# Keeping the split input-projection weights of a decoder layer in DRAM after the first token tile

## The chip, the cores and the metric

The kernel runs on one core of a Trainium2 chip. The metric is the device time of one execution in microseconds (us). A core has five engines, each with an instruction stream of its own that runs in order: TensorE (PE in the profile, its weight loads PEld), VectorE (DVE), ScalarE (ACT), GpSimd (POOL) and SyncE (SP), which here issues nearly all DMAs between DRAM and the on-chip memories. Streams meet at semaphores. An instruction that waits holds up everything behind it in its own stream, and for SP that means every later DMA.

## The reference, cut to what matters

The reference is one decoder layer on 2048 tokens of width 1024, in float32. What the change touches is the input projection; what follows it is shown so that the stages can be named.

```python
mod = c_act @ w_ada[l] + b_ada[l]
shift_a, scale_a, gate_a, shift_f, scale_f, gate_f = jnp.split(mod[:, None, :], N_MOD, axis=-1)
h = x * (1.0 + scale_a) + shift_a
proj = h @ w_in                       # (2048, 1024) @ (1024, 3088)
sb_q, sb_k, sb_v, g_q, g_k, g_v, g_lr, g_r = jnp.split(proj, split_at, axis=-1)
# group A: stick-breaking attention, 8 heads x 64
w = jnp.where(causal, jnp.exp(log_beta + tail), 0.0)
# group B: gated linear attention, 4 heads, chunks of 64
o = jnp.concatenate([o_sb, o_gla], axis=-1) @ w_out
x = layer_norm(DEEPNORM_ALPHA * x + (1.0 + gate_a) * o, ln1_g, ln1_b)
h = x * (1.0 + scale_f) + shift_f
x = layer_norm(DEEPNORM_ALPHA * x + (1.0 + gate_f) * conv_glu_ffn(h), ln2_g, ln2_b)
```

## The kernel before

**Products in two parts.** Every float32 operand of a large product is split into a high part, rounded to the matmul's format, and a low part, which is the rest. A product is then three matmuls into one PSUM bank: high by high, high by low, low by high (`col_tile`, L267 to L269, with the weights stationary, and `row_tile`, L276 to L278, with the tokens stationary).

**How a weight is split.** `weights` (L162) loads up to 1024 elements a partition of a weight (four blocks of 128 rows by 256 columns, 512 KB) into a tile `w_raw`, of which there are three. `split` (L156) has ACT copy it to `w_hi` with a cast (L158) and POOL subtract to make `w_lo` (L159, engine `pool`). ACT, DVE and POOL instructions that go through the helper `Urgent` carry line L101 in the profile. `ring_pair` (L147) hands out the pairs `w_hi`, `w_lo`: four pairs that are used in turn, so a pair is written again when the matmuls that read it are done. A 256-column group of `w_in` takes two pairs.

**Tiles and stages.** The 2048 tokens go in four tiles of 512. For each tile the whole of `w_in` is loaded and split: 11 groups of 256 columns in two parts each and one group of 272 columns in three (`C_GV + 256` to `C_LR + 16`), 25 parts a tile and 100 in all. Tile 0's projections (`projections(0)`, L806) stand at the start, beside the sums that make shift and scale from `w_ada`. Then `attend(t)` (L471), the stick-breaking attention of tile t, is interleaved with `between(t)`: the linear attention of tile t (`gla`, L543, with its own four groups of `w_in`), the gate (`gla_gate`, L677) and the projections of tile t+1 (`proj_sb`, L435). `spread` (L789) decides by costs such as `WP` how far the one goes for each step of the other. Beside them run the rest of the `w_ada` sums (`ada_rest`, L280, on DVE) and `scale_w_out` (L307), which makes both parts of `w_out` and stores them in DRAM; `load_w_out` (L319) later loads them straight into ring pairs. The last attention runs beside the output projection (`mixer_out`, L721). The feed-forward part starts near 1,600 us and its order stands apart from `w_in`.

**The attention step** works on 128 queries by 512 keys: two matmuls (L494, L495), two sigmoids on ACT (L496, L497), a scan on DVE (L508), a product on DVE or POOL (L510), four transposes on PE (L518), a cast on ACT (L522), a subtraction on DVE (L523) and two matmuls (L524, L526).

**What sets the order.** The program is written stage by stage, and a scheduler then places every instruction in its engine's stream by a timeline that it estimates. A change in the durations or the number of instructions moves rows on all engines as far as the stages allow.

Of the kernel before, what the change touches and what calls it, by code (L numbers as in the profile page):

```python
# [19 lines left out]
F32 = mybir.dt.float32  # L20
# [8 lines left out]
P = 128  # L29
TQ = 512  # L30
NB = TQ // P
D = 1024
KT = D // P
# [49 lines left out]
C_SBQ, C_SBK, C_SBV, C_GQ, C_GK, C_GV, C_LR, C_GR = 0, 512, 1024, 1536, 1792, 2048, 2560, 2576  # L83


def layer(tc, x, c, w_ada, b_ada, w_in, gla_w_gate, gla_b_gate, sb_norm_g, gla_norm_g, w_out,
          ln1_g, ln1_b, w_ff_gate, w_ff_up, conv_w, conv_b, w_down, ln2_g, ln2_b, out):
    nc = tc.nc
# [15 lines left out]
    act, dve, pool = Urgent(nc.scalar), Urgent(nc.vector), Urgent(nc.gpsimd)  # L104
# [3 lines left out]
    w_ada, w_in, w_out = w_ada[0], w_in[0], w_out[0]  # L108
# [6 lines left out]
    dram = ctx.enter_context(tc.tile_pool(name="dram", bufs=1, space=DRAM))  # L115
# [31 lines left out]
    def ring_pair():  # L147

        pool, size = ext.get("pool"), ext.get("size", 0)
        i = ext.get("i", 0)  # L150
        ext["i"] = (i + 1) % (4 + size)
        if i < 4:
            return [wring.tile([P, 1024], F32R, name=f"w_{n}", bufs=4) for n in ("hi", "lo")]
        return [pool.tile([P, 1024], F32R, name=f"w_{n}x", bufs=size) for n in ("hi", "lo")]

    def split(raw, n, nw, lo_eng):  # L156
        hi, lo = (w[:, 0:1024 // nw * nw].rearrange("p (k c) -> p k c", c=nw) for w in ring_pair())
        act.copy(hi[:, 0:n], raw[:, 0:n])  # L158
        lo_eng.tensor_sub(lo[:, 0:n], raw[:, 0:n], hi[:, 0:n])  # L159
        return hi, lo  # L160

    def weights(src, lo_eng, nk=KT, scale=None):  # L162

        nw = src.shape[-1]
        per = 1024 // nw
        parts = []
        for k0 in range(0, nk, per):
            n = min(per, nk - k0)
            raw = wring.tile([P, 1024], F32, name="w_raw", bufs=3)
            raw = raw[:, 0:per * nw].rearrange("p (k c) -> p k c", c=nw)  # L170
            nc.sync.dma_start(raw[:, 0:n], src[k0 * P:(k0 + n) * P, :].rearrange("(k p) c -> p k c", p=P))
            if scale is not None:
                pool.tensor_mul(raw[:, 0:n], raw[:, 0:n], scale.unsqueeze(1).to_broadcast([P, n, nw]))
            parts.append(split(raw, n, nw, lo_eng))
        return parts

    def load_x(t):
        xt = []
        for tb in range(NB):
            xx = pj.tile([P, D], F32, name="t4k", bufs=4)  # L180
            nc.sync.dma_start(xx, x[t * TQ + tb * P:t * TQ + (tb + 1) * P, :])
            xt.append(xx)
        return xt

    with tc.tile_pool(name="ada", bufs=1, reuse_waits="tile") as ada:
# [34 lines left out]
        w_first = [[], []]  # L220
        done = 0
        for n in FIRST:
            ada_cols(KT + done, n, wa_first if done == 0 else None)
            ada_cols(done, n)
            cs = slice(done * P, (done + n) * P)
            for tb in range(NB):
                nc.sync.dma_start(x_first[tb][:, cs], x[tb * P:(tb + 1) * P, cs])
            if done % 4 == 0 and (done == 0 or not WLATE):
                for w, c0 in zip(w_first, (C_SBQ, C_SBK)):
                    w += weights(w_in[done * P:(done + 4) * P, c0:c0 + 256], pool, 4)  # L230
            done += n
        if WLATE:
            for w, c0 in zip(w_first, (C_SBQ, C_SBK)):
                w += weights(w_in[512:D, c0:c0 + 256], pool, 4)
        gmask_f = ada.tile([P, P], F32, name="gmask_f")
        nc.vector.memset(gmask_f, 1.0)
        nc.gpsimd.affine_select(gmask_f, gmask_f, pattern=[[1, P]], compare_op=ALU.is_ge, fill=0.0,
# [197 lines left out]
    def proj_sb(t, h):  # L435
        hh, hl = h
        for g in range(2):
            for kind, c0, dst in (("q", C_SBQ, dq), ("k", C_SBK, dk)):
                first = t + g == 0
                w = w_first[c0 // 512] if first else weights(w_in[:, c0 + 256 * g:c0 + 256 * (g + 1)], pool)  # L440
                for half in range(2):
                    if first:
                        ps = ps_first.pop(0)
                    else:
                        ps = psm.tile([P, TQ], F32, name="acc", bufs=3)
                        col_tile(ps, w, half, hh, hl)
                    hi = pj.tile([P, TQ], F32R, name="ev_hi", bufs=2)
                    lo = pj.tile([P, TQ], F32R, name="ev_lo", bufs=2)
                    if kind == "q":
                        act.mul(hi, ps, 0.125)  # L450
                        dve.scalar_tensor_tensor(lo, ps, 0.125, hi, ALU.mult, ALU.subtract)
                    else:
                        act.copy(hi, ps)
                        dve.tensor_sub(lo, ps, hi)
                    p = 2 * g + half
                    nc.sync.dma_start(dst[p][t][0], hi.bitcast(F32))
                    nc.sync.dma_start(dst[p][t][1], lo.bitcast(F32))
                    yield WP
            w = weights(w_in[:, C_SBV + 256 * g:C_SBV + 256 * (g + 1)], pool)
            for tb in range(NB):  # L460
                ps = psm.tile([P, TQ], F32, name="acc", bufs=3)
                row_tile(ps[:, 0:256], w, tb, hh, hl)
                v2 = pj.tile([P, 4, P], F32R, name="ev_v", bufs=2)
                pv = ps[:, 0:256].rearrange("p (h d) -> p h d", d=64)
                act.copy(v2[:, :, 0:64], pv)
                dve.tensor_sub(v2[:, :, 64:P], pv, v2[:, :, 0:64])
                nc.sync.dma_start(dv[g][t][:, tb], v2.bitcast(F32))
                if tb % 2:
                    yield WP
# [73 lines left out]
    def gla(t, h):  # L543
        hh, hl = h
        vn = pj.tile([P, NB, 512], F32, name="vn")
        w = weights(w_in[:, C_GV + 256:C_LR + 16], pool)
        for tb in range(NB):
            ps = psm.tile([P, TQ], F32, name="acc", bufs=3)
            row_tile(ps[:, 0:272], w, tb, hh, hl)
# [4 lines left out]
        with tc.high_priority(offset=400):  # L554
# [12 lines left out]
            m = pj.tile([P, 2, TQ], F32, name="t4k", bufs=4)  # L567
# [7 lines left out]
            act.activation(m, u, AF.Exp, scale=1.0 / 16)  # L575
            act.activation(u, u, AF.Exp, scale=-1.0 / 16)
        eb, enb = m, u
        w = weights(w_in[:, C_GV:C_GV + 256], pool)
        for tb in range(NB):
            ps = psm.tile([P, TQ], F32, name="acc", bufs=3)  # L580
            row_tile(ps[:, 0:256], w, tb, hh, hl)
            act.copy(vn[:, tb, 0:256], ps[:, 0:256])
            if tb % 2:
                yield WP
        wq = weights(w_in[:, C_GQ:C_GQ + 256], pool)
        wk = weights(w_in[:, C_GK:C_GK + 256], pool)
        cores = []
        for g in range(2):
            ps = psm.tile([P, TQ], F32, name="acc", bufs=3)
# [87 lines left out]
    def gla_gate(t, h, heads):  # L677
        hh, hl = h
        for hd in heads:
            if hd % 2 == 0:  # L680
                w = weights(w_in[:, C_GR + P * hd:C_GR + P * hd + 256], pool)
            ps = psm.tile([P, TQ], F32, name="acc", bufs=3)
            col_tile(ps, w, hd % 2, hh, hl)
            sg = pj.tile([P, TQ], F32, name="t2k", bufs=2)
            act.activation(sg, ps, AF.Sigmoid)
            dve.scalar_tensor_tensor(sg, ps, cols[:, R_GLG + hd:R_GLG + hd + 1], sg, ALU.mult, ALU.mult)
            nc.sync.dma_start(dsr[hd][t], sg)
            yield WP
# [416 lines left out]
    first = len(units) - NFF  # L1105
# [105 lines left out]
```

## Time and profile before

| | us |
|---|---|
| median of 3 runs (lowest, highest) | 3020.49 (3019.66, 3026.47) |
| the profiled execution's own time | 3018.13 |
| its span, first to last instruction | 3016.4 |
| its mean granted TensorE clock | 0.955 |

The page of the profile gives busy time by engine, the span in 40 slices of 75.4 us, DMA queues, the chain of waits that ended last, groups of instructions and DMA issues. A group's row reads: line, engine, operation, what it writes and reads, partitions by elements, count, busy us and mean ns of one, and after a second bar, where there is one, how long the engine stood idle just before these instructions and who ended that. A row of a windows table reads: from and to in us, length, busy us of each engine with its count of instructions, granted clock, mean busy share of the 16 DMA engines, GB/s. Times of a stretch are counted from the span's start.

### The profile page before, as it was taken

How to read it: one execution, taken by the hardware profiler on the slowest of the kernel's cores; microseconds unless marked ns; L12 is line 12 of the kernel's file. 1: busy time of each engine (PE TensorE's matmuls, PEld its weight loads, DVE VectorE, ACT ScalarE, POOL GpSimd, SP SyncE). 2: the span in 40 equal slices, each digit the busy share in tenths (PEclk: the TensorE clock that was granted, in tenths of full speed). 3: DMA queues.
4: the chain of work that ended last, by engine and by line, in shares of the span. 5: the costliest groups of instructions: out<-in, count | busy, mean ns of one | idle time of the engine just before them, and what ended most of it. 6: DMA issues, size and time to landing. Idle time of an engine off the chain costs nothing.

```text
span 3016.4 us, 37763 instructions
## 1 busy us (share of the span) xinstructions
PE 2789.2 (92%) x13387; PEld 2246.3 (74%) x13387; DVE 2060.3 (68%) x2829; ACT 1168.0 (39%) x1910; POOL 1219.6 (40%) x1202
## 2 busy tenths in 40 slices
PE   7998999989898998989886999988999997999998
PEld 6877877777787775667655788876888886888887
DVE  6466568688888779798547776767666665335665
ACT  2544354475566656544212333333222333112111
POOL 3554345477585545465425434453343430000000
PEclk9998999999999998988988999999999998999999
DMA  7755555546464335557763244344222336444553
GB/s 248 229 174 178 160 156 153 187 147 180 133 216 123 91 121 174 182 185 232 249 227 96 80 129 130 91 133 126 81 81 84 84 98 227 131 131 157 168 169 128
DMA packets 364710, 457.48 MB, mean 152 GB/s; under 512 B 21518, under 2 KB 257256, under 8 KB 364520
## 3 DMA queue, kind: packets, MB, share of 16 engines
q1 hardware_dynamic: 362216, 446.66, 47.7%
q0 software_dynamic: 2304, 8.39, 0.7%
q8 instruction: 106, 1.74, 0.2%
q14 instruction: 84, 0.69, 0.1%
HBM read 356.39 MB, written 98.57 MB: 151 GB/s over the span
## 4 chain that ended last, share of the span: by engine, by line
PE 66%; DVE 18%; DMA 5%; issue 4%; ACT 3%; POOL 2%; SPq 1%; POOLq 0%; DVEq 0%; ACTq 0%
PE acc L396 6%; PE acc L394 6%; PE acc L395 6%; DVE pp L508 5%; PE acc L974 4%; PE acc L972 4%; PE acc L973 4%; PE acc L101 3%; PE acc L268 3%; PE acc L267 3%; PE acc L269 2%; PE wt L518 2%; PE wt L972 2%; PE wt L973 2%; PE wt L974 2%
## 5 line engine op out<-in xcount | busy, mean ns | idle before, releaser
L508 DVE TENSOR_TENSOR_SCAN pp<-pp,beta 128x512 f32<-128x512 f32 (+2 forms) x320 | 408.8, 1291 | 55.7 <-ACT beta L497 27.5
L101 POOL TENSOR_TENSOR w_lo<-w_raw,w_hi 128x1024 fp32r<-128x1024 f32 (+2 forms) x108 | 265.1, 2460 | 256.1 <-ACT w_hi L101 230.6
L101 ACT CAST w_hi<-w_raw 128x512 fp32r<-128x512 f32 (+3 forms) x248 | 201.4, 830 | 353.3 <-PE acc L973 87.3
L510 POOL TENSOR_TENSOR beta<-beta,pp 128x512 f32<-128x512 f32 (+2 forms) x160 | 200.2, 1252 | 244.2 <-DVE pp L508 205.6
L101 POOL TENSOR_TENSOR w_lo<-wsum,w_hi 128x1024 fp32r<-128x1024 f32 x80 | 207.0, 2587 | 220.3 <-ACT w_hi L101 192.5
L972 PE MATMUL acc<-t,w_hi 128*128 128x512 f32 x640 | 251.2, 394 | 22.9 <-ACT t L101 21.3
L974 PE MATMUL acc<-t,w_lo 128*128 128x512 f32 x640 | 247.3, 393 | 8.0 <-DVE w_lo L101 8.0
L973 PE MATMUL acc<-t,w_hi 128*128 128x512 f32 x640 | 251.5, 393 | 1.6 <-DVE t L101 1.4
L394 PE MATMUL acc<-t,ah 128*128 128x512 f32 x576 | 225.2, 391 | 16.3 <-ACT ah L101 16.3
L523 DVE TENSOR_TENSOR wl<-wt,wh 128x512 fp32r<-128x512 f32 (+1 forms) x320 | 185.4, 597 | 65.0 <-ACT wh L522 63.3
L101 ACT CAST ah<-al 128x1408 fp32r<-128x1408 f32 x64 | 88.1, 1377 | 363.5 <-PE acc L395 359.6
L396 PE MATMUL acc<-t,al 128*128 128x512 f32 x576 | 225.2, 391 | 0.4 <-DVE al L101 0.4
L395 PE MATMUL acc<-t,ah 128*128 128x512 f32 x576 | 225.0, 391 | 0.0
L522 ACT CAST wh<-wt 128x512 fp32r<-128x512 f32 (+1 forms) x320 | 162.1, 530 | 158.7 <-PE wt L518 146.7
L496 ACT ACTIVATE pp<-z 128x512 f32<-128x512 f32 (+2 forms) x320 | 173.8, 544 | 124.7 <-PE z L495 58.6
L518 PE MATMUL wt<-ident,beta 128*128 128x128 f32 x1088 | 189.1, 294 | 13.2 <-DVE beta L510 8.5
L267 PE MATMUL acc<-hh,w_hi 128*128 128x512 f32 x480 | 194.7, 406 | 4.8 <-DVE ev_lo L101 2.5
L268 PE MATMUL acc<-hl,w_hi 128*128 128x512 f32 x480 | 191.5, 399 | 3.4 <-DVE hl L101 3.4
L269 PE MATMUL acc<-hh,w_lo 128*128 128x512 f32 x480 | 190.9, 398 | 1.9 <-POOL w_lo L101 1.9
L526 PE MATMUL o_ps<-wl,v 128*128 128x512 f32 (+1 forms) x320 | 136.6, 431 | 45.6 <-DVE wl L523 42.7
L497 ACT ACTIVATE beta<-z 128x512 f32<-128x512 f32 (+2 forms) x320 | 172.0, 544 | 14.4 <-PE wt L518 14.3
L518 PEld LDWEIGHTS wt<-ident,beta 128*128 128x128 f32 x1088 | 144.8, 151 | 43.9 <-DVE beta L510 10.6
(289 smaller groups left out, 7228.1 us busy)
## 6 DMA issues: line engine op xcount, KB each, us to landing
w_raw<-in_w_in_dram SPq DMA_DIRECT2D x88, 512.0 KB
al<-da SPq DMA_DIRECT2D x64, 704.0 KB
w_raw<-in_w_ff_gate_dram SPq DMA_DIRECT2D x48, 512.0 KB
w_raw<-in_w_ff_up_dram SPq DMA_DIRECT2D x48, 512.0 KB
k<-dk SPq DMA_DIRECT2D x160, 128.0 KB
v<-dv SPq DMA_DIRECT2D x80, 256.0 KB
da<-cv SPq DMA_DIRECT2D x40, 512.0 KB
q<-dq SPq DMA_DIRECT2D x128, 128.0 KB
```

The source lines that it names most:

```text
L101: return f(*args, **kw)
L267: nc.tensor.matmul(ps, hi[:, k % 4, cs], xh[k], start=(k == 0), stop=False)
L268: nc.tensor.matmul(ps, hi[:, k % 4, cs], xl[k], start=False, stop=False)
L269: nc.tensor.matmul(ps, lo[:, k % 4, cs], xh[k], start=False, stop=(k == nk - 1))
L394: eng.matmul(ps, xh[k][:, ts], hi[:, i % 2, :], start=(first and i == 0), stop=False)
L395: eng.matmul(ps, xh[k][:, ts], lo[:, i % 2, :], start=False, stop=False)
L396: eng.matmul(ps, xl[k][:, ts], hi[:, i % 2, :], start=False, stop=(last and k == min(len(xh), k0 + 2 * len(w)) - 1))
L508: nc.vector.tensor_tensor_scan(pp[:, 0:n][:, ::-1], pp[:, 0:n][:, ::-1], beta[:, 0:n], first, ALU.mult, ALU.bypass)
L518: pe.transpose(wt[:, i * P:(i + 1) * P], ws[i][:, ks], ident)
L972: nc.tensor.matmul(ps, w[0][:, k, :], t[k][:, 0, :], start=first and k == 0, stop=False, **add)
L973: nc.tensor.matmul(ps, w[0][:, k, :], t[k][:, 1, :], start=False, stop=False, **add)
L974: nc.tensor.matmul(ps, w[1][:, k, :], t[k][:, 0, :], start=False, stop=k == 3, **add)
```

## The change

A dictionary `dwi` and a function `w_in_cols` take the place of `weights` at all uses of `w_in`. The first call for a group of columns (tile 0) splits as before and then stores both parts, each as a DRAM tensor of 128 partitions by 4 x 256, by two DMAs on SP. A later call (tiles 1 to 3) takes the next ring pair and loads both parts into it. No cast and no subtraction stands there any more. The first two groups are kept in two halves, as tile 0 makes them.

```diff
+    dwi = {}
+
+    def w_in_cols(c0, n, k0=0, nk=KT):
+        key = c0, k0
+        if key not in dwi:
+            parts = weights(w_in[k0 * P:(k0 + nk) * P, c0:c0 + n], pool, nk)
+            dwi[key] = []
+            per = 1024 // n
+            for i, hl in enumerate(parts):
+                m = min(per, nk - i * per)
+                kept = [dram.tile([P, m, n], F32, name=f"dwi{c0}_{k0}_{i}{j}") for j in "hl"]
+                for w, d in zip(hl, kept):
+                    nc.sync.dma_start(d, w[:, 0:m].bitcast(F32))
+                dwi[key].append(kept)
+            return parts
+        parts = []
+        for kept in dwi[key]:
+            m = kept[0].shape[1]
+            hl = [w[:, 0:1024 // n * n].rearrange("p (k c) -> p k c", c=n) for w in ring_pair()]
+            for w, d in zip(hl, kept):
+                nc.sync.dma_start(w[:, 0:m].bitcast(F32), d)
+            parts.append(hl)
+        return parts
...
-                w = w_first[c0 // 512] if first else weights(w_in[:, c0 + 256 * g:c0 + 256 * (g + 1)], pool)
+                w = w_first[c0 // 512] if first else (
+                    [*w_in_cols(c0, 256, 0, 4), *w_in_cols(c0, 256, 4, 4)] if g == 0 else w_in_cols(c0 + 256, 256))
...
-            w = weights(w_in[:, C_SBV + 256 * g:C_SBV + 256 * (g + 1)], pool)
+            w = w_in_cols(C_SBV + 256 * g, 256)
```

The other uses (the two loops that fill `w_first`, four groups in `gla`, one in `gla_gate`) change in the same way. Lines of the changed kernel are 25 to 27 higher than those of before: the scan of L508 is L534 there, the stores stand in L190 and the reloads in L198.

The instructions of each engine stand as follows. POOL, beside an attention of the middle tiles, before (`w_lo<-w_raw` is the subtraction of `split`, `w_raw<-w_raw,ada_acc` a step of `scale_w_out`, the others belong to the attention):

```order
L510 TENSOR_TENSOR beta<-beta,pp 128x384
L101 TENSOR_TENSOR w_lo<-w_raw,w_hi 128x1024
L507 COPY pp<-pp 128x1
L510 TENSOR_TENSOR beta<-beta,pp 128x512
L507 COPY pp<-pp 128x1
L101 TENSOR_TENSOR w_lo<-w_raw,w_hi 128x1024 x2
L315 TENSOR_TENSOR w_raw<-w_raw,ada_acc 128x1024
L507 COPY pp<-pp 128x1
L510 TENSOR_TENSOR beta<-beta,pp 128x512
L507 COPY pp<-pp 128x1
L101 TENSOR_TENSOR w_lo<-w_raw,w_hi 128x1024 x2
```

and POOL in a comparable place of the changed kernel:

```order
L536 TENSOR_TENSOR beta<-beta,pp 128x384
L101 TENSOR_TENSOR w_lo<-w_raw,w_hi 128x1024
L533 COPY pp<-pp 128x1
L536 TENSOR_TENSOR beta<-beta,pp 128x512
L533 COPY pp<-pp 128x1 x2
L101 TENSOR_TENSOR w_lo<-w_raw,w_hi 128x1024
L536 TENSOR_TENSOR beta<-beta,pp 128x512
L533 COPY pp<-pp 128x1 x2
L340 TENSOR_TENSOR w_raw<-w_raw,ada_acc 128x1024
```

The subtractions that are left there are those of `scale_w_out`; over the program POOL has 75 subtractions fewer and ACT 75 casts fewer.

SP, in the first tile, before (`wa` are tiles of `w_ada`, `dq` and `dk` the projections that go out to DRAM):

```order
L171 DMA w_raw<-in_w_in_dram 128x4x256 x2
L189 DMA wa_216<-in_w_ada_dram 128x4x256 x2
L189 DMA wa_234<-in_w_ada_dram 128x4x256 x2
L171 DMA w_raw<-in_w_in_dram 128x4x256 x4
L456 DMA dq_0_300<-ev_hi 128x512
```

and in the changed kernel:

```order
L190 DMA dwi_0_0h<-w_hi 128x1024 x2
L190 DMA dwi_0_0l<-w_lo 128x1024
L171 DMA w_raw<-in_w_in_dram 128x4x256
L190 DMA dwi_0_0l<-w_lo 128x1024
L171 DMA w_raw<-in_w_in_dram 128x4x256
L214 DMA wa_224<-in_w_ada_dram 128x4x256 x2
L190 DMA dwi_4_0h<-w_hi 128x1024
L214 DMA wa_242<-in_w_ada_dram 128x4x256 x2
L190 DMA dwi_4_0l<-w_lo 128x1024
L171 DMA w_raw<-in_w_in_dram 128x4x256
```

Two stores of 512 KB now stand ahead of most of the raw loads of tile 0. The store of a low part waits for POOL's subtraction, and the raw load behind it waited for a subtraction already.

SP in the projections of tile 1, before, with what each row waits for (`DMAHW` is the landing of an earlier DMA, `Pool`, `PE`, `DVE`, `Activation` an engine; `k`, `q` are tiles of the attention):

```order
L171 DMA w_raw<-in_w_in_dram 128x4x256 [waits DMAHW3_49,DVE_49]
L456 DMA dk_1_317<-ev_hi 128x512 [waits DMAHW4_49,Activation_49]
L478 DMA q_3987<-dq_1_301 64x512 [waits DMAHW5_49]
L457 DMA dk_1_317<-ev_lo 128x512 [waits DMAHW6_49,DVE_49]
L478 DMA q_3987<-dq_1_301 64x512 [waits DMAHW7_49]
L478 DMA q_3987<-dq_1_301 64x512 [waits DMAHW0_49]
L484 DMA k_3458<-dk_1_317 64x512 [waits DMAHW4_49,DMAHW1_49]
L484 DMA k_3684<-dk_0_316 64x512 [waits DMAHW2_49]
L171 DMA w_raw<-in_w_in_dram 128x4x256 [waits DMAHW3_49,Pool_49]
```

and in the changed kernel:

```order
L198 DMA w_hi<-dwi_0_0h 128x1024 [waits DMAHW2_49,PE_49]
L198 DMA w_lo<-dwi_0_0l 128x1024 [waits DMAHW3_49,PE_49]
L504 DMA q_4045<-dq_1_317 64x512 [waits DMAHW4_49]
L198 DMA w_hi<-dwi_0_1h 128x1024 [waits DMAHW5_49,PE_49]
L198 DMA w_lo<-dwi_0_1l 128x1024 [waits DMAHW6_49,PE_49]
L482 DMA dk_1_337<-ev_hi 128x512 [waits DMAHW7_49,Activation_49]
L483 DMA dk_1_337<-ev_lo 128x512 [waits DMAHW0_49,DVE_49]
L510 DMA k_3534<-dk_1_333 64x512 [waits DMAHW1_49]
```

A load of `w_in` waited for POOL or DVE to be done with a raw tile; a reload waits for PE to be done with the ring pair, and the attention's loads stand behind it. In PE's stream the last 5,659 of 12,921 instructions stand in the same order as before; they are the feed-forward part.

More of the change, by code (lines that the diff above doesn't have):

```diff
@@ L229, in layer @@
                 for w, c0 in zip(w_first, (C_SBQ, C_SBK)):
-                    w += weights(w_in[done * P:(done + 4) * P, c0:c0 + 256], pool, 4)
+                    w += w_in_cols(c0, 256, done, 4)
             done += n
@@ L233, in layer @@
             for w, c0 in zip(w_first, (C_SBQ, C_SBK)):
-                w += weights(w_in[512:D, c0:c0 + 256], pool, 4)
+                w += w_in_cols(c0, 256, 4, 4)
         gmask_f = ada.tile([P, P], F32, name="gmask_f")
@@ L545, in gla @@
         vn = pj.tile([P, NB, 512], F32, name="vn")
-        w = weights(w_in[:, C_GV + 256:C_LR + 16], pool)
+        w = w_in_cols(C_GV + 256, 272)
         for tb in range(NB):
@@ L577, in gla @@
         eb, enb = m, u
-        w = weights(w_in[:, C_GV:C_GV + 256], pool)
+        w = w_in_cols(C_GV, 256)
         for tb in range(NB):
@@ L584, in gla @@
                 yield WP
-        wq = weights(w_in[:, C_GQ:C_GQ + 256], pool)
-        wk = weights(w_in[:, C_GK:C_GK + 256], pool)
+        wq = w_in_cols(C_GQ, 256)
+        wk = w_in_cols(C_GK, 256)
         cores = []
@@ L680, in gla_gate @@
             if hd % 2 == 0:
-                w = weights(w_in[:, C_GR + P * hd:C_GR + P * hd + 256], pool)
+                w = w_in_cols(C_GR + P * hd, 256)
             ps = psm.tile([P, TQ], F32, name="acc", bufs=3)
```

## The prediction

> **What bounds the kernel now.** I read the page first, then the windows table, then the chain of waits and the groups of the stretch in which `w_in` is used. On the page:
>
> ```profile
> span 3016.4 us, 37763 instructions
> PE 2789.2 (92%) x13387; PEld 2246.3 (74%) x13387; DVE 2060.3 (68%) x2829; ACT 1168.0 (39%) x1910; POOL 1219.6 (40%) x1202
> PE   7998999989898998989886999988999997999998
> PE 66%; DVE 18%; DMA 5%; issue 4%; ACT 3%; POOL 2%; SPq 1%; POOLq 0%; DVEq 0%; ACTq 0%
> ```
>
> PE looks full, and POOL is 2% of the chain: at first sight POOL's work is free. The stages differ, so I cut out the start, where tile 0 is projected (its 25 raw loads are issued up to 168.4 us), and the stretch of tiles 1 to 3 (the last of 100 at 1025.8 us). First the raw loads up to 169 and up to 1130 us, then the windows table:
>
> ```profile
> L171 SPq DMA_DIRECT2D w_raw<-in_w_in_dram x25: 367/389/897, 10.6 to 168.4; - x25
> L171 SPq DMA_DIRECT2D w_raw<-in_w_in_dram x100: 367/384/1270, 10.6 to 1025.8; - x100
> 20.00:180.00 160.00, 149.69 (x869) 129.09 (x867) 91.27 (x143) 69.31 (x120) 77.71 (x79) 0.99 0.71 223
> 160.00:1030.00 870.00, 797.42 (x4494) 660.84 (x4493) 648.74 (x855) 462.41 (x864) 494.94 (x579) 0.94 0.52 159
> ```
>
> In the last row PE is busy for 797 of 870 us, yet the clock is granted at 0.94 only, and DVE is busy for 649 us. Here DVE is a second bound. The groups of DVE, POOL and ACT in that stretch show it:
>
> ```profile
> L508 DVE TENSOR_TENSOR_SCAN pp<-pp,beta 128x512 f32<-128x512 f32 x131 | 203.9, 1571 | 17.8 <-ACT beta L497 14.5 <-POOL beta L501 3.1
> L510 DVE TENSOR_TENSOR beta<-beta,pp 128x512 f32<-128x512 f32 x76 | 82.6, 1089 | 2.2
> L523 DVE TENSOR_TENSOR wl<-wt,wh 128x512 fp32r<-128x512 f32 x124 | 81.9, 679 | 32.2 <-ACT wh L522 32.2
> L289 DVE SCALAR_TENSOR_TENSOR ada_acc<-w_raw,c_act,ada_acc 128x256 f32<-128x256 f32 x98 | 64.0, 653 | 1.6
> L101 POOL TENSOR_TENSOR w_lo<-w_raw,w_hi 128x1024 fp32r<-128x1024 f32 x75 | 191.5, 2558 | 139.0 <-ACT w_hi L101 124.6 <-DMA k<-dk 9.9 <-ACT wh L522 4.5
> L101 POOL TENSOR_TENSOR w_lo<-w_raw,w_hi 128x816 fp32r<-128x816 f32 x6 | 11.9, 1976 | 18.4 <-ACT w_hi L101 17.9 <-DMA dwo1l<-w_lo 0.6
> L101 ACT CAST w_hi<-w_raw 128x1024 fp32r<-128x1024 f32 x75 | 78.8, 1056 | 72.1 <-PE acc L268 42.1 <-DMA w_raw<-in_w_in_dram 21.5 <-POOL w_raw L315 3.8
> ```
>
> The scan's mean is 1.57 us, but an undisturbed scan is far shorter. Three rows of the timeline, DVE's and then POOL's:
>
> ```profile
> 641.84 1.27 DVE L508 TENSOR_TENSOR_SCAN pp<-pp,beta 128x512 f32<-128x512 f32 x1
> 649.47 3.42 DVE L508 TENSOR_TENSOR_SCAN pp<-pp,beta 128x512 f32<-128x512 f32 x1
> 648.95 2.87 POOL L101 TENSOR_TENSOR w_lo<-w_raw,w_hi 128x1024 fp32r<-128x1024 f32 x1
> ```
>
> The same scan takes 1.27 us or 3.42 us. The long one met a subtraction that ended at 648.95 + 2.87 = 651.82, and itself ended 1.07 us later: it stood still until POOL was done. The other two groups have a wide range for equal shapes, 0.39 to 2.9 us:
>
> ```profile
> L510 DVE TENSOR_TENSOR beta<-beta,pp x160: 390/680/2892, 112.2 to 1437.2; 128x512 f32<-128x512 f32 x128, 128x256 f32<-128x256 f32 x32
> L289 DVE SCALAR_TENSOR_TENSOR ada_acc<-w_raw,c_act,ada_acc x112: 447/485/2621, 109.8 to 579.4; 128x256 f32<-128x256 f32 x112
> ```
>
> So POOL's subtractions are paid on DVE, under DVE's name.
>
> The Trainium skill, page "SBUF — State Buffer", section "Who interferes with whom", says that a DVE instruction with two SBUF inputs contends with a GpSimd instruction that reads SBUF, and that the loser blocks for the other's whole length. The 3.42 us agree. By that rule all of DVE's excess hangs on POOL, which is the upper end below.
>
> **The change, part by part.** It is summed against the profiled execution, 3018.13 us (span 3016.4 us and 1.73 us around it); the median is 2.36 us higher, and I add that at the end.
>
> *Work that goes.* Tiles 1 to 3 lose 75 casts and 75 subtractions. By the 128x1024 rows that is at most 75 x 2.56 = 192 us of POOL's 495 and 75 x 1.06 = 79 us of ACT's 462; nine smaller ones make it a little less.
>
> *POOL and ACT on the chain.* The chain of waits by line, from 160 to 400 us, from 600 to 800 and over the whole stretch:
>
> ```profile
> by line: DVE pp L508 8.4%; PE acc L267 7.7%; PE acc L268 7.5%; PE acc L269 7.4%; PE acc L276 4.3%; PE acc L278 4.2%; PE acc L277 4.2%; issue 3.8%; PE acc L671 3.5%; DVE beta L510 3.4%; POOL w_lo L101 2.9%; DVE t4k L101 2.7%; PE acc L667 2.5
> by line: DVE pp L508 16.9%; issue 6.5%; PE wt L518 5.7%; PE acc L671 4.9%; PE acc L267 3.9%; PE acc L268 3.8%; PE z L494 3.7%; PE acc L269 3.6%; DVE wl L523 3.5%; PE o_ps L526 3.2%; PE z L495 3.0%; POOL w_lo L101 3.0%; PE acc L667 3.0%; DVE
> by line: DVE pp L508 11.2%; PE acc L267 6.9%; PE acc L268 6.9%; PE acc L269 6.8%; issue 5.8%; PE wt L518 4.9%; DVE beta L510 4.0%; PE o_ps L526 3.3%; PE acc L671 3.2%; PE o_ps L524 2.9%; PE acc L276 2.9%; PE acc L277 2.8%; PE acc L278 2.8%;
> ```
>
> POOL's `w_lo` has 2.9% of 240 us and 3.0% of 200 us, 7 + 6 = **13 us**, of which nearly all goes. ACT works between PE and DVE: L523 above waited 32.2 us for the casts of L522. The 79 us that go are 17% of ACT's 462, so I take 17% of 32.2, **5 us**, between 0 and all 32.
>
> *DVE's stalls.* Their sum in the stretch: the scans 131 x (1571 - 1270) ns = 39 us, the products 76 x (1089 - 680) = 31, the sums 98 x (653 - 485) = 16, together 87 us. POOL's other reading work stays and stalls too. The subtractions have 203 of POOL's 495 us, 41%, so 36 us of the 87 are theirs, and 75 of some 84 (81 in the rows above, and three smaller) go: 32 us. A second measure is the stretch after the last subtraction, where the same attention runs beside the output projection:
>
> ```profile
> L508 DVE TENSOR_TENSOR_SCAN pp<-pp,beta 128x512 f32<-128x512 f32 x65 | 97.4, 1510 | 13.9 <-ACT beta L497 13.0 <-POOL beta L501 0.7
> L510 DVE TENSOR_TENSOR beta<-beta,pp 128x512 f32<-128x512 f32 x34 | 32.5, 957 | 0.3
> ```
>
> Scans take 1510 there and products 957: 131 x 61 + 76 x 132 ns = 18 us less. DVE's work thus shrinks by 18 to 32 us. What of it is on the path? Scan and product have 11.2 + 4.0 = 15.2% of the chain of 870 us, 132 us, of at least 287 us that the two groups are busy, so about 45%; but an instruction that stalls is late, and so stands on the chain more often than its share. Bounds are 45% of 18, 8 us, and all 32; I take **20 us**.
>
> *The reloads.* Tiles 1 to 3 load 150 parts where they loaded 75 raw ones, and they cannot start before PE frees the ring pair. The nearest rows are the reloads of `w_out`, which go the same way into the same ring:
>
> ```profile
> L324 SPq DMA_DIRECT2D w_hi<-dwo1h x16: 360/421/1489, 1270.5 to 1576.4; - x16
>   PE acc L101: 1.9, 3
>   PE acc L394: 1.4, 1
> ```
>
> PE stood idle for 1.9 + 1.4 = 3.3 us behind 64 such loads; 150/64 of it is 8 us. They fill the whole ring at once, though, and a group of `w_in` fills half of it, so that PE has the other group, 48 matmuls, to do meanwhile. Worse is what the chain has of them where no attention runs beside:
>
> ```profile
> 1467.31 5.37 DMA w_hi<-dwo1h
> 1472.75 10.63 DMA w_hi<-dwo1h
> 1571.89 5.22 DMA w_hi<-dwo1h
> ```
>
> That is 21 us, without cover. Here the attention covers them; I take **3 us**, between 0 and 21. Behind a waiting reload on SP stand the attention's `k`, `q` and `v`; their tiles are two or three deep.
>
> *The stores at the start.* Tile 0 stores 22 x 2 x 512 + 2 x 2 x 408 + 2 x 272 = 24,704 KB, 25.3 MB, from its first splits until some 10 us after the raw load at 168.4 us. The 20 to 180 row above moved 223 GB/s x 160 us = 35.7 MB, so 61.0 MB would be due in 160 us, 381 GB/s. What the DMA engines have shown in 20 us:
>
> ```profile
> 5.00:25.00 20.00, 12.04 (x49) 11.19 (x50) 14.42 (x19) 3.90 (x8) 4.70 (x2) 1.00 1.07 372
> 20.00:40.00 20.00, 19.51 (x86) 16.27 (x85) 15.44 (x28) 7.61 (x12) 9.07 (x4) 1.00 0.96 301
> 80.00:100.00 20.00, 20.00 (x118) 17.74 (x117) 2.93 (x5) 5.60 (x9) 9.31 (x5) 1.00 1.08 333
> ```
>
> At 372 GB/s the 61.0 MB take 164 us, 4 us more; at 333 GB/s 183, 23 us more; at 301 GB/s 203, 43 us more. PE is busy for 150 of these 160 us, so little of a delay finds room, but raw loads are issued ahead of need (three tiles), which hides the first part of a backlog. I take **8 us**, between 0 and 43. What is late next there is a raw load of `w_in` or the attention's first `q` and `k`.
>
> The Trainium skill, page "DMA: Bandwidth & Descriptors", section "Specifications", speaks against this part: it puts HBM at about 358 GB/s for a core. The 372 GB/s of the trace are above that, and the measurement decides; by the page's figure the estimate would be 61.0/358 = 170 us, 10 us more.
>
> *The clock.* It was 0.94 in the stretch. If PE's idle time shrinks it may rise, worth up to 6% of 870, 52 us; if reloads make PE wait it may fall. I take 0.
>
> *The feed-forward part* keeps PE's order: 0.
>
> **Sum:** -13 - 5 - 20 + 3 + 8 = -27 us, 2991 us for the profiled execution and, with 2.36 us, **2994 us**.
>
> **The rivals.**
>
> *More is gained.* All 32 us of DVE, 13 of POOL and 10 of ACT go, the start costs 4 us, and the clock returns a quarter of its 52: -64, 2957 us. For it speaks that scan and product are the chain's first entries; against it, that PE is busy for 797 of 870 us and takes over as the bound.
>
> *No difference.* PE is the bound after all: its waits in the stretch are 870 - 797 = 73 us in many small pieces, and another releaser is ready behind each. Then the 27 us come to less than 9 either way: 3020 us.
>
> *DMA becomes the bound, slower.* The place is the first 180 us and then SP's stream. The stores queue ahead of raw loads, 43 us at 301 GB/s, the 20 to 40 row, and the reloads cost 21 us, as on the chain of `w_out`. Against the 38 us gained that is +26: 3047 us. It decides from the point where the start costs more than the 35 us that are left of the gain, a rate under 61.0 MB / 195 us = 313 GB/s. For it speak the 1.08 DMA share in the 80 to 100 row already; against it, that a 0.71 share on the mean leaves room between the peaks.
>
> **How the numbers follow.** Chances: forecast 0.50, more 0.14, no difference 0.16, slower 0.20. A measurement of this kernel tells 0.3%, 9 us, from no change. Of the forecast's 0.50 some 0.02 falls inside that. Faster is 0.62, same 0.18, slower 0.20. The range takes in the larger gain with some of the clock, 2950 us, and half of the slower case, 3032 us, past the point where the start's cost cancels the gain.
>
> **What would show it.** POOL's busy time falls to about 1,035 us and ACT's to about 1,090 us; the scan's mean between 160 and 1030 us falls from 1571 to 1500 ns or less; `w_lo` leaves the chain; the 20 to 180 row rises to some 350 GB/s at a PE busy share near 150 us; PE waits little for a `w_hi<-dwi`. I am wrong if the scan's mean stays (the rest of POOL's work fills in), if PE waits for reloads by tens of us, or if the mark at which the first attention ends moves out by more than 30 us.

## The result, and the profile after

| | us |
|---|---|
| before, median of 4 runs (lowest, highest) | 3022.70 (3019.66, 3026.47) |
| after, median of 4 runs (lowest, highest) | 2998.32 (2995.74, 3005.14) |
| ratio, 95% interval | 0.9921, 0.9902 to 0.9940 |
| the profiled execution of after, its span | 2996.83, 2994.5 |

The change saves 24 us (18 to 30 by the interval), against 27 forecast. The lines of the page that answer to those shown of before:

```profile
span 2994.5 us, 37777 instructions
PE 2785.5 (93%) x13387; PEld 2247.3 (75%) x13387; DVE 2006.5 (67%) x2829; ACT 1097.0 (37%) x1834; POOL 1015.3 (34%) x1127
```

POOL lost 204 us of busy time, ACT 71 and DVE 54, with the same 2,829 instructions on DVE: DVE got faster without being touched. PE does the same work. The two stretches of the prediction, in the windows table:

```profile
20.00:180.00 160.00, 142.34 (x795) 125.17 (x794) 87.25 (x136) 70.50 (x130) 71.03 (x93) 0.90 0.91 314
160.00:1030.00 870.00, 828.94 (x4708) 688.08 (x4709) 614.18 (x898) 412.51 (x823) 317.96 (x527) 0.96 0.67 219
```

They went opposite ways. In the first, PE began 795 matmuls where it had begun 869, and was granted 0.90 of its clock instead of 0.99. In the second it was busy for 829 us instead of 797 and took 214 matmuls more. DVE's groups in the second stretch of the changed kernel are:

```profile
L534 DVE TENSOR_TENSOR_SCAN pp<-pp,beta 128x512 f32<-128x512 f32 x138 | 193.0, 1417 | 24.8 <-ACT beta L523 17.9 <-POOL beta L527 4.2 <-POOL pp L529 2.4
L536 DVE TENSOR_TENSOR beta<-beta,pp 128x512 f32<-128x512 f32 x80 | 72.8, 910 | 2.6
L549 DVE TENSOR_TENSOR wl<-wt,wh 128x512 fp32r<-128x512 f32 x131 | 86.7, 677 | 44.7 <-ACT wh L548 44.4
L314 DVE SCALAR_TENSOR_TENSOR ada_acc<-w_raw,c_act,ada_acc 128x256 f32<-128x256 f32 x105 | 53.1, 506 | 1.7
```

The scan fell from 1571 to 1417 ns, the product from 1089 to 910, the `w_ada` sum from 653 to 506. Four marks that stand at the same places of the program say where the time came from: the 34th matmul of the attention's scores, the issue of the first reload of `w_out`'s first half, and of its second half's first and last. Before, then after:

```profile
L494 PE MATMUL z<-k,q x34: 221/376/794, 104.5 to 282.7; 128*128 128x128 f32 x9, 128*128 128x256 f32 x9, 128*128 128x384 f32 x8, 128*128 128x512 f32 x8
L324 SPq DMA_DIRECT2D w_hi<-dwo0h x16: 360/374/539, 1068.9 to 1537.4; - x16
```

```profile
L520 PE MATMUL z<-k,q x34: 220/334/776, 106.7 to 301.3; 128*128 128x128 f32 x9, 128*128 128x256 f32 x9, 128*128 128x384 f32 x8, 128*128 128x512 f32 x8
L349 SPq DMA_DIRECT2D w_hi<-dwo0h x16: 359/376/717, 1040.0 to 1518.1; - x16
L349 SPq DMA_DIRECT2D w_hi<-dwo1h x16: 380/421/1145, 1249.8 to 1556.9; - x16
```

The first mark came 18.6 us later (282.7 to 301.3), the second 28.9 us earlier (1068.9 to 1040.0), the third 20.7 us earlier (1270.5, shown in the prediction, to 1249.8), the last 19.5 us earlier (1576.4 to 1556.9). PE's last matmul with a weight of `w_in` moved from 1125.4 to 1098.4, 27.0 us earlier, which bears out the second mark. So the start lost 19 us, the stretch behind it gained 47, the last attention gave 9 back, and the feed-forward part behind it stayed.

### The profile page after: what moved, and what is told of

Read it like the earlier page. It is cut to its first block, busy times and chain, and to the rows that moved or that the text cites. A ratio compares the mean times of both kernels' runs of the same rounds, so it can differ in the third digit from the quotient of the medians.

```text
span 2994.5 us, 37777 instructions
## 1 busy us (share of the span) xinstructions
PE 2785.5 (93%) x13387; PEld 2247.3 (75%) x13387; DVE 2006.5 (67%) x2829; ACT 1097.0 (37%) x1834; POOL 1015.3 (34%) x1127
## 4 chain that ended last, share of the span: by engine, by line
PE 46%; DVE 8%; DMA 3%; issue 2%; POOL 1%; ACT 1%; SPq 0%; POOLq 0%; DVEq 0%; ACTq 0%
PE acc L419 6%; PE acc L421 6%; PE acc L420 6%; PE acc L1000 4%; PE acc L998 4%; PE acc L999 4%; PE acc L101 3%; PE wt L998 2%; PE wt L999 2%; PE wt L1000 2%; DVE cv L1090 1%; DVE pp L534 1%; DVE w_lo L101 1%; PE z L998 1%; PE z L999 1%
## 5 line engine op out<-in xcount | busy, mean ns | idle before, releaser
L534 DVE TENSOR_TENSOR_SCAN pp<-pp,beta 128x512 f32<-128x512 f32 (+2 forms) x320 | 389.3, 1232 | 61.9 <-POOL beta L527 34.3
L101 ACT CAST w_hi<-w_raw 128x512 fp32r<-128x512 f32 (+2 forms) x173 | 125.3, 746 | 262.9 <-PE acc L999 85.8
L101 DVE TENSOR_TENSOR w_lo<-w_raw,w_hi 128x512 fp32r<-128x512 f32 (+1 forms) x140 | 127.6, 934 | 49.5 <-PE acc L1000 27.2
```

Of the source, the lines that this page charges most:

```text
L101: return f(*args, **kw)
L534: nc.vector.tensor_tensor_scan(pp[:, 0:n][:, ::-1], pp[:, 0:n][:, ::-1], beta[:, 0:n], first, ALU.mult, ALU.bypass)
```

## The experiments

The theory was that POOL's subtractions had held DVE's instructions, so that their removal is the gain, and that the stores cost part of it at the start. The main rivals were that something else in the reloading kernel makes the gain (other order, less work on ACT, a less occupied POOL), and that the reloads themselves cost. Each ratio is against the kernel before (medians 3020 to 3024 us). Where two kernels are compared, it is by these ratios; the change stands at 0.9921.

### The stores alone

Tile 0 stores both parts, and the later tiles load and split as before.

```diff
-        parts = []
-        for kept in dwi[key]:
-...
-        return parts
+        return weights(w_in[k0 * P:(k0 + nk) * P, c0:c0 + n], pool, nk)
```

> Tile 0 stores both parts as in the change, but tiles 1 to 3 load w_in and split it again as before; what is stored is read by nobody. Theory A (the 25.3 MB of stores fill the DMA queues in the first 230 us and delay the start by some 20 us): 10 to 25 us slower than before, 3032 to 3047 us, and the 20 to 180 us row of the windows table above 290 GB/s. Theory B (the late start of the change comes from the new order of the program, not from the stores' traffic): within 5 us of before.

Measured: 3037.04 us, ratio 1.0055 (1.0040 to 1.0071), 16.5 us slower than before.

```profile
20.00:180.00 160.00, 141.98 (x805) 123.77 (x804) 88.52 (x137) 70.76 (x131) 72.15 (x93) 0.94 0.93 316
L527 DVE TENSOR_TENSOR_SCAN pp<-pp,beta 128x512 f32<-128x512 f32 x124 | 193.5, 1576 | 19.9 <-ACT beta L516 13.9 <-POOL pp L522 3.2 <-POOL beta L520 2.7
```

The windows row is that of the changed kernel again (PE 142 us, 316 GB/s), while the scan's mean in the later stretch is as long as before. The 34th matmul of the scores starts at 302.4 us here, as late as in the changed kernel. The stores explain the lost start and nothing of the gain.

### The reloads alone

Only the first part is stored, and all reloads read it.

```diff
-            dwi[key] = []
...
+            if not dwi:
+                dwi["one"] = [dram.tile([P, 1024], F32, name=f"dwi_{j}") for j in "hl"]
+                for w, d in zip(parts[0], dwi["one"]):
+                    nc.sync.dma_start(d.rearrange("p (k c) -> p k c", c=n), w.bitcast(F32))
...
+            for w, d in zip(hl, dwi["one"]):
+                nc.sync.dma_start(w[:, 0:m].bitcast(F32), d[:, 0:m * n].rearrange("p (k c) -> p k c", c=n))
```

> Tile 0 stores one part alone (two DMAs); tiles 1 to 3 reload that one part 75 times in place of their own weights, so the values are not the layer's, but the reloads have the sizes and forms of the change. Theory A: the start is as before, and the gain between 200 and 1050 us stands alone: 15 to 25 us faster than the change, 2973 to 2984 us. Theory B: as the change, 2995 to 3003 us.

Measured: 2988.46 us, 0.9892 (0.9862 to 0.9922), 33 us faster than before (24 to 42 by the interval).

```profile
20.00:180.00 160.00, 149.06 (x861) 128.91 (x861) 89.43 (x139) 68.06 (x117) 78.49 (x77) 0.99 0.74 227
L532 DVE TENSOR_TENSOR_SCAN pp<-pp,beta 128x512 f32<-128x512 f32 x140 | 190.8, 1382 | 28.5 <-ACT beta L521 24.0 <-POOL beta L525 3.9
```

The start is that of before and the scans are short. The gain without the stores is a little smaller than was expected. The two parts of the change add up to -33 + 16.5 = -16 us, against -24 measured; the intervals are wide enough for both, so the sum is not contradicted, but it is not confirmed closely either.

### One part kept, the other made again

First the low part is kept, and tiles 1 to 3 load the raw weight and cast it; then the high part is kept, and they subtract.

```diff
...
+            act.copy(hi[:, 0:m], raw[:, 0:m])
+            nc.sync.dma_start(lo[:, 0:m].bitcast(F32), d)
...
```

> The low part alone is kept: tiles 1 to 3 load w_in, cast it on ACT as before, and reload the low part; POOL's 75 subtractions are gone, ACT's 75 casts stay, the stores are half. Theory A (the gain is POOL's subtractions, which hold DVE up): most of the gain stays and the start costs half, 2985 to 3002 us, scan mean from 160 to 1030 us near 1420 ns. Theory C (the gain is the casts that no longer stand ahead of the attention's work on ACT): 3012 to 3030 us.

Measured: 2995.85 us, 0.9921 (0.9897 to 0.9946), scan 1424 ns.

```diff
...
+            nc.sync.dma_start(hi[:, 0:m].bitcast(F32), d)
+            pool.tensor_sub(lo[:, 0:m], raw[:, 0:m], hi[:, 0:m])
...
```

> The high part alone is kept: tiles 1 to 3 reload it, load w_in and subtract on POOL as before; ACT's 75 casts are gone, POOL's 75 subtractions stay, the stores are half. Theory A: little or none of the gain, and half the start's cost, 3012 to 3035 us, scan mean near 1570 ns. Theory C: 2990 to 3005 us.

Measured: 3055.99 us, 1.0112 (1.0081 to 1.0144), scan 1599 ns, much slower than expected. The first windows row is of the kernel with the low part kept, the next of that with the high part kept, and the last is from the latter's waits on POOL between 160 and 1030 us (total us, times, longest):

```profile
20.00:180.00 160.00, 152.17 (x869) 132.19 (x867) 90.09 (x142) 68.42 (x118) 78.01 (x76) 0.97 0.89 288
```

```profile
20.00:180.00 160.00, 152.64 (x869) 132.74 (x867) 90.91 (x142) 69.83 (x121) 75.93 (x77) 0.98 0.90 291
POOL w_lo L101 <- DMA w_hi<-dwi: 103.1, 21, 13.2
```

Without subtractions the gain is there, casts or not; with them it isn't. Half of the stores, 12.7 MB, cost little at the start: PE starts 869 matmuls as before, at 288 GB/s, and the 34th score of the kernel with the low part kept is 4 us late (286.5). What made the second kernel slower than before was not foreseen: the subtraction now waits for a reload, and POOL's stream runs in order, so the attention's work on POOL stood behind it for 103 us.

### POOL reading, POOL writing

To the changed kernel, work is added on POOL for each reloaded part, with results that nothing uses. First a real subtraction of the two reloaded parts:

```diff
+            pool.tensor_sub(raw[:, 0:m], hl[1][:, 0:m].bitcast(F32), hl[0][:, 0:m].bitcast(F32))
```

> The change, and for each of the 75 reloaded parts POOL subtracts the reloaded high part from the low part into a raw tile that nobody reads: the subtractions are back in number, size and place, but no matmul depends on them. Theory A (POOL's subtractions cost by holding DVE up and by standing ahead of POOL's own attention work): the gain between 200 and 1050 us is given back, 3020 to 3045 us, scan mean from 160 to 1030 us near 1570 ns. Theory E (what counted was that the matmuls no longer wait for a low part made late): 2998 to 3008 us.

Measured: 3060.79 us, 1.0118 (1.0103 to 1.0133), above both expectations. It has the same fault as the kernel with the high part kept: its subtractions waited 118 + 20 us for the two reloads (`w_lo<-dwi_0l` and `w_lo<-dwi_1l` on POOL), so it doesn't isolate the reads. The next two wait for no reload, only for a free raw tile: between 160 and 1030 us POOL stood idle until DVE's `w_ada` sums freed one, 58 us in the first of them and 70 in the second. Memsets that occupy POOL about as long:

```diff
+            for k in (m, m, m - m // 2):
+                pool.memset(raw[:, 0:k], 0.0)
```

> As the run with the subtractions put back, but POOL fills the raw tile by three memsets of together about 2.4 us, which read nothing from SBUF. Theory A1 (DVE is held up by POOL's reads): the scan mean stays near 1420 ns and the time near the change, 2998 to 3012 us. Theory A2 (it is POOL's in-order stream: 2.4 us of anything ahead of the attention's masks and products delays them): as with the subtractions, within 8 us of that run.

and a subtraction whose operands are a constant tile:

```diff
+            r = rmask[:, 0:n].unsqueeze(1).to_broadcast([P, m, n])
+            pool.tensor_sub(raw[:, 0:m], r, r)
```

> As the run with the subtractions put back, but POOL subtracts a constant tile from itself (two reads of SBUF, 128x1024, about 2.4 us) into the raw tile, so it never waits for a reload. Theory A1 (POOL's reads hold DVE up): 3020 to 3045 us, scan mean from 160 to 1030 us 1500 ns or more, at POOL's busy time of the fill run. Theory A3 (the run with the subtractions put back lost its time because POOL waited for reloads in front of the attention's work): as the fill run, 3000 to 3014 us, scan mean near 1440 ns.

Measured: with memsets 3006.98 us, 0.9942 (0.9920 to 0.9964); with reads 3034.27 us, 1.0039 (1.0020 to 1.0058). The window and DVE's two groups, of the memsets and then of the reads:

```profile
160.00:1030.00 870.00, 819.99 (x4665) 679.88 (x4664) 609.64 (x885) 406.95 (x809) 488.05 (x741) 0.96 0.67 219
L537 DVE TENSOR_TENSOR_SCAN pp<-pp,beta 128x512 f32<-128x512 f32 x135 | 192.4, 1442 | 28.2 <-ACT beta L526 20.2 <-POOL beta L530 5.4 <-POOL pp L532 2.4
L539 DVE TENSOR_TENSOR beta<-beta,pp 128x512 f32<-128x512 f32 x79 | 72.0, 913 | 3.2 <-POOL pp L532 0.9
```

```profile
160.00:1030.00 870.00, 805.13 (x4511) 667.51 (x4510) 633.08 (x856) 391.50 (x779) 460.54 (x572) 0.94 0.65 212
L537 DVE TENSOR_TENSOR_SCAN pp<-pp,beta 128x512 f32<-128x512 f32 x128 | 202.7, 1599 | 22.0 <-ACT beta L526 14.8 <-POOL beta L530 4.7 <-POOL pp L532 2.4
L539 DVE TENSOR_TENSOR beta<-beta,pp 128x512 f32<-128x512 f32 x75 | 80.8, 1078 | 2.6
```

POOL is busier with the memsets (488 us, before the change it was 495) than with the reads (461), yet the scan stays at 1442 ns there and goes back to 1599 here, and so does the product; the `w_ada` sum goes back only in part, from 507 to 551 ns (653 before). One scan of each kernel with its neighbour on POOL, DVE's row first:

```profile
430.92 1.28 DVE L537 TENSOR_TENSOR_SCAN pp<-pp,beta 128x512 f32<-128x512 f32 x1
429.94 1.96 POOL L101 MEMSET w_raw<- 128x1024 f32 x2
```

```profile
507.50 2.91 DVE L537 TENSOR_TENSOR_SCAN pp<-pp,beta 128x512 f32<-128x512 f32 x1
507.26 2.07 POOL L101 TENSOR_TENSOR w_raw<-rmask 128x1024 f32<-128x1024 f32 x1
```

The scan beside a memset takes its undisturbed time; the scan beside a reading subtraction lasts 1.08 us past the subtraction's end at 509.33. At like occupancy the reads cost 0.0097 of the time, 29 us, more than the memsets, with intervals that stay apart. In the windows rows PE is idle for 65 us of the 870 with the reads and for 50 with the memsets, and a matmul takes 178.5 against 175.8 ns on the mean, which is another 12 us. And with the reads added the change stands where the stores alone had put the kernel (1.0039 against 1.0055, with intervals that overlap): the reads are enough to undo the gain, though no matmul waits for their results. Whether the memsets cost anything (0.9942 against 0.9921) these runs can't tell. The Trainium skill, page "SBUF — State Buffer", section "Who interferes with whom", says that a DVE instruction with two SBUF inputs contends with a GpSimd instruction that reads SBUF and not with one that only writes it; 1599 against 1442 ns agree.

### The casts alone

To the changed kernel, one ACT copy of a constant tile is added for each reloaded part.

```diff
+            act.copy(raw[:, 0:m], rmask[:, 0:n].unsqueeze(1).to_broadcast([P, m, n]))
```

> The change, and ACT copies a constant tile into a raw tile once for each of the 75 reloaded parts (128x1024, about 1.06 us, never waiting for a reload): the casts' load on ACT is back and nothing depends on it. The prediction's term (5 us): 2999 to 3009 us. Rival (ACT's casts are a large part of the gain): 3010 to 3025 us. Third (nothing): 2994 to 2999 us.

Measured: 3003.76 us, 0.9935 (0.9911 to 0.9960), 4 us over the change by the ratios. The attention's subtraction on DVE, whose row of the changed kernel stands above, waits longer for ACT:

```profile
L551 DVE TENSOR_TENSOR wl<-wt,wh 128x512 fp32r<-128x512 f32 x131 | 86.7, 677 | 53.3 <-ACT wh L550 53.3
```

53.3 us against 44.7. The intervals of 0.9935 and 0.9921 overlap, so the runs agree with the 5 us of the prediction without separating them from nothing; 32 us, its upper end, they exclude.

### The stores from ACT's queue

```diff
-                    nc.sync.dma_start(d, w[:, 0:m].bitcast(F32))
+                    nc.scalar.dma_start(d, w[:, 0:m].bitcast(F32))
```

> The change with tile 0's 50 stores issued from ACT's queue instead of SP's. Theory A (the start is late because 25.3 MB of stores fill the DMA engines): no gain, 2996 to 3010 us. Rival (the stores that wait in SP's stream hold up the loads behind them): the start is on time and the run is near the reload-only run, 2984 to 2992 us.

Measured: 3025.51 us, 1.0006 (0.9996 to 1.0016). The change's whole gain is gone, and neither expectation held. The start's row, the longest single wait of ACT and of PE there, and one kind of the stores on ACT's queue:

```profile
20.00:180.00 160.00, 130.00 (x731) 112.42 (x729) 77.42 (x117) 62.79 (x112) 60.21 (x71) 0.91 0.85 287
ACT w_hi L101 <- DMA wg_raw<-in_gla_w_gate_dram: 11.8, 1, 11.8
PE o_ps L237 <- ACT s1a L241: 9.7, 2, 9.4
L190 ACTq DMA_DIRECT2D dwi_0l<-w_lo x14: 326/348/547, 33.4 to 240.8; - x14
```

Each of the 50 stores takes ACT's queue some 0.33 us. The first of them is issued at 31.45 us: ACT's stream stood there until a transfer that SP had issued, that of `wg_raw`, had landed, and ACT was idle for 11.8 us. Behind the store stood a cast and the scale that PE needed, and PE waited 9.4 us. The rest of the 26 us by which this kernel is slower than the change is not explained. SP's stream was the better place: what stood behind a store there is a later transfer, here it is PE's next operand.

### The stores spread over two tiles

Tile 0 stores the low parts only. Tile 1 loads the raw weight once more, casts it, reloads the low part and stores the high one; tiles 2 and 3 reload both.

```diff
...
+            if second:
+                act.copy(hi[:, 0:m], raw[:, 0:m])
+            else:
+                nc.sync.dma_start(hi[:, 0:m].bitcast(F32), dhi)
+            nc.sync.dma_start(lo[:, 0:m].bitcast(F32), dlo)
+            if second:
+                nc.sync.dma_start(dhi, hi[:, 0:m].bitcast(F32))
...
```

> The low parts are stored by tile 0, the high parts by tile 1, which casts them on ACT once more and reloads the low parts; tiles 2 and 3 reload both. The stores of the first 230 us are halved. Theory A: start as with the low part alone (some 3 us late), later gain nearly that of the reload-only run: 2985 to 2995 us, faster than the change by 4 to 13 us. Rival (the traffic between 200 and 500 us now delays the second tile): 2996 to 3005 us.

Measured: 2973.07 us (2969.84 to 2985.23), 0.9825 (0.9807 to 0.9842), faster than before and after, and 29 us under the change by the ratios (0.9825 against 0.9921).

```profile
20.00:180.00 160.00, 152.06 (x869) 132.47 (x867) 89.69 (x142) 68.00 (x116) 76.89 (x76) 0.97 0.88 289
160.00:1030.00 870.00, 831.19 (x4743) 688.10 (x4741) 612.86 (x907) 441.64 (x860) 315.00 (x534) 0.96 0.70 226
```

The start is whole again (869 matmuls, the 34th score at 283.6 us) and the later stretch keeps the gain. That would give the change's time less the 16.5 us that the stores cost alone. The other 12 or so were not expected, and it leads even the kernel with the reloads alone, by 20 us. Two more kernels are made to find out why. One is the same without the stores, its reloads reading one part; the other has the stores and the same order of work on PE and POOL, and only its reloads' address is one for all.

```diff
...
+            dhi, dlo = (d[:, 0:m * n].rearrange("p (k c) -> p k c", c=n) for d in dwi["one"])
...
```

> The run whose high parts are stored by tile 1, without its stores (one part is stored, all reloads read that one, so the values are not the layer's): tile 1 loads w_in, casts it and reloads a low part, tiles 2 and 3 reload both. If the form of tile 1 is what made that run faster than the reload-only run: 2965 to 2978 us. If it was not, as the reload-only run: 2983 to 2993 us.

```diff
...
+            one = dwi["lo"].rearrange("p k c -> p (k c)")[:, 0:m * n].rearrange("p (k c) -> p k c", c=n)
...
+                nc.sync.dma_start(hi[:, 0:m].bitcast(F32), one)
+            nc.sync.dma_start(lo[:, 0:m].bitcast(F32), one)
```

> The program and the order of the run in which the second tile casts the high part again, with its stores; only the address that the reloads read is one stored low part for all of them, so the values are not the layer's. If repeated reads of one place are what kept the two kinds of run without stores from being as fast as that one: 2988 to 3000 us. If not (then it is their order of work, or the stores themselves): 2970 to 2980 us.

Measured: 2995.88 us, 0.9919 (0.9888 to 0.9950), and 2982.15 us (2970.99 to 2983.95), 0.9866 (0.9850 to 0.9883). The first lies above both of its expectations, the second between its two. The lead is thus not the form of the second tile, since the first of the two has it without the lead. The one address explains little: the two kernels with the same order have nearly the same lowest and highest times, though by the ratios 12 us lie between them. What is left is that the order of the whole program differs, as the schedule is made anew for each kernel. That was not shown; it stays open. It also limits the other comparisons: 12 us between two kernels whose work stands in one order, and 20 between others, are unexplained, so differences such as the 4 us of the casts or the 6 of the memsets show nothing by themselves, and the 29 us of the reads count because DVE's durations move with them.

## Why the prediction held, point by point

**The sum** was right (-27 us forecast, -24 measured), but the terms of tiles 1 to 3 together and that of the stores were each too small by about 10 us, in opposite directions, and a term for the last attention was missing. That the sum came so near is in part luck.

**DVE's stalls.** The mechanism was right, by the kernels with memsets and reads. The size was too low: at the counts of before, 131 x 154 + 76 x 179 + 98 x 147 ns = 48 us went from the three groups, where 18 to 32 were forecast. How they reached PE is shown by PE's waits between 160 and 1030 us (total us, times, longest). The longest row, before and then after:

```profile
PE o_ps L526 <- DVE wl L523: 19.5, 19, 2.1
PE o_ps L552 <- DVE wl L549: 10.3, 8, 3.0
```

All waits together were 73 us before and 41 after. The rows that DVE ended add up to 54 and then 27 us, those of ACT to 15 and 11, those of POOL to 3 and 0.4. So some 27 us came to PE through DVE, where 20 were taken: the subtraction `wl`, itself not slowed, stands behind scans and products in DVE's stream. The step that was mis-sized is the share: by busy time the subtractions were 41% of POOL's work, but they had 48/87 = 55% of the stalls. A share by time takes each microsecond of POOL to hold DVE alike, and the memsets show that it doesn't.

**POOL and ACT on the chain.** The 5 us of ACT agree with the 4 that the casts cost when added back, a difference too small to tell from nothing. The 13 us of POOL weren't measured apart: the chain of waits of the changed kernel breaks off in the middle (its shares add up to 61%), so whether `w_lo` left it can't be read. PE's own waits speak against a term of that size: before the change only 3 us of them were ended by POOL, 1.8 of these by a `w_lo`. What the chain put down to POOL may have been passed on by other engines. All four terms of tiles 1 to 3 together, -13 - 5 - 20 + 3 = -35, were -47 by the marks.

**The reloads.** 3 us were forecast. PE waited for none: among those who waited for the reloads' line there is only one wait of ACT, 5.0 us. PE did wait once for a `k` of the attention, 2.2 us just before the first mark, and once for a `q`, 0.8 us, which it had not done before between 160 and 1030 us; whether a reload held these up isn't shown.

**The stores at the start.** 8 us were forecast and 0 to 43 kept open; 16.5 us were measured by the stores alone and 18.6 at the mark. The step that was mis-sized is how much of a delay stays hidden, "raw loads are issued ahead of need (three tiles), which hides the first part of a backlog". One window of 20 us of before, then three of the changed kernel and its raw loads of tile 0:

```profile
40.00:60.00 20.00, 17.48 (x102) 14.97 (x102) 15.46 (x24) 4.56 (x8) 6.28 (x4) 1.00 0.46 145
```

```profile
40.00:60.00 20.00, 13.95 (x64) 11.26 (x62) 14.96 (x20) 4.80 (x7) 7.73 (x3) 0.81 1.06 393
80.00:100.00 20.00, 20.00 (x89) 16.53 (x89) 2.74 (x5) 5.47 (x8) 8.62 (x4) 1.00 1.05 385
100.00:120.00 20.00, 18.69 (x143) 17.60 (x141) 9.20 (x13) 10.38 (x24) 11.33 (x24) 1.00 1.05 378
L171 SPq DMA_DIRECT2D w_raw<-in_w_in_dram x25: 378/432/1197, 10.5 to 210.9; - x25
```

The traffic did fill the troughs (393 GB/s where 145 had flowed, at a DMA share of 1.06), but not all of them, since the mean came to 314 and not to the 350 expected. The last raw load was issued 42 us later (168.4 to 210.9), the upper end of that term; more than half of it was hidden, and 18.6 us reached the attention. The price per byte isn't even: by the first mark the first 12.7 MB cost 1 to 4 us (283.6 and 286.5 against 282.7; 291.2 in the kernel with the high part kept, where POOL waits too), the second 12.7 MB the rest.

**The clock** was put at 0. It rose from 0.94 to 0.96 in the later stretch and fell from 0.99 to 0.90 at the start, where a matmul took 142.34/795 = 179 ns on the mean instead of 172: 795 x 7 ns, 5 to 6 of the start's 18.6 us. In the later stretch it took 828.94/4708 = 176.1 ns instead of 177.4, some 6 us less. Both are estimates, as the mix of shapes is not quite the same; together they come to the 0 that was put down, by cancelling out.

**The feed-forward part** took 3016.4 - 1576.4 = 1440.0 us before and 2994.5 - 1556.9 = 1437.6 after, nearly the 0 forecast. The missing term is the last attention, which gave back 9 us; why it is longer now stays open.

**The rivals.** The slower one had the right place and a price about right for the transfers, but it took their lateness for PE's. Its point, a rate under 313 GB/s, was all but reached (314), and the kernel still gained 24 us. "No difference" fell with the 47 us between the marks and with PE's waits, which shrank by 32 us: another releaser did not stand ready behind each. "More is gained" had 55 us and 13 of the clock for tiles 1 to 3 and a price of 4 for the start; they gave 47, and the start cost 19.

## What to carry to other kernels

An engine that is far from full, and nearly absent from the chain of waits, can still be the dear one: look for equal instructions of another engine with a wide range of durations, find the neighbour that each long one outlasts, and count that neighbour's removal there. Work that is kept for later use needs its stores spread to where transfers have room; half of them in the next tile made this kernel some 29 us faster still, of which about 16 are what the stores alone cost and the rest is not explained. A computation on an engine in the middle of the attention must not wait for a transfer that comes in just in time, and a store is best issued from a stream in which only transfers stand behind it.

## What the runs showed of the hardware

The attention's subtraction `wl<-wt,wh`, which takes one operand from the transposes' PSUM tile, never stalled. Its row over the whole program before the change (minimum, median, maximum in ns):

```profile
L523 DVE TENSOR_TENSOR wl<-wt,wh x320: 255/674/693, 117.9 to 1449.2; 128x512 fp32r<-128x512 f32 x128, 128x256 fp32r<-128x256 f32 x32
```

It reaches 693 ns at most, where the product of two on-chip tiles of the same shape reached 2892. So it kept its 679 and 677 ns while its neighbours in the table fell.

A wait of PE can cost more than its length. In the changed kernel:

```profile
53.65 0.28 PE L303 MATMUL acc<-w_hi,hl 128*128 128x256 f32 x1
...
58.87 0.59 PE L239 MATMUL o_ps<-ones,acc 128*128 128x1 f32 x2 [3.46 <-DVE acc L234]
...
60.34 0.56 PE L301 MATMUL acc<-w_hi,hh 128*128 128x256 f32 x1
```

PE waited 3.46 us for a sum of `w_ada`, and a matmul of the shape that had taken 0.28 us took 0.56 us behind it. The windows row of 40 to 60 us shown above has a granted clock of 0.81, where before the change it was 1.00. The Trainium skill, page "TensorE: Matmul & The Clock Gate", section "Part 1: The HAM clock gate", says that the array falls to half its clock after an idle window of about 3.4 us; the wait and the doubled duration agree. So long a wait is not the only thing that came before slow matmuls, though:

```profile
41.47 0.39 PE L294 MATMUL wt<-hh,w_lo 128*128 128x512 f32 x1
...
46.55 0.63 PE L293 MATMUL z<-hl,w_hi 128*128 128x512 f32 x1
```

Between these two PE had waited only 0.64, 0.43 and 1.17 us, and from 45 to 50 us the granted clock was 0.66. What lowered it there isn't shown.
